# First stage of a two-layer diffusion step: small loads on ScalarE's queue, large loads reordered, first modulation and norm given priority

## The chip, the cores and the metric

The kernel runs on one core of one Trainium2 chip. The time is device microseconds of one execution; the median of several is given. The five engines of the core are named as in the profile: PE (TensorE, matmuls; its weight loads are PEld), DVE (VectorE), ACT (ScalarE), POOL (GpSimd) and SP (SyncE). SP only issues transfers. ACT, too, can issue transfers, from its own instruction stream and into a queue of its own.

## What is computed

One inference step of a hybrid network, two layers, float32, on 128 context tokens and 256 latent tokens of 1024 features (the two streams, 384 token columns together). Cut to what matters here:

```python
def trunk_layer(x, cond, lp, ctx_cache, rope_a, rope_b):
    mod = (jax.nn.silu(cond) @ lp["w_mod"] + lp["b_mod"])[:, None, :]
    sh1, sc1, g1, sh2, sc2, g2 = jnp.split(mod, MOD_CHUNKS, axis=-1)
    h = rms_norm(x, lp["norm1"]) * (1 + sc1) + sh1
    o, new_ctx = token_mixers(h, lp, ctx_cache, rope_a, rope_b)
    x = x + g1 * o
    h = rms_norm(x, lp["norm2"]) * (1 + sc2) + sh2
    x = x + g2 * conv_ffn(h, lp)
    return x, new_ctx
...
h = jnp.sin(freq[0] * (z @ w1 + b1))
h = jnp.sin(freq[1] * (h @ w2 + b2))
h = (h @ w3).reshape(L, 2, HY_ORDER, HY_CH)
```

`token_mixers` has two attentions and a long convolution (Hyena) behind one projection `w_in`. The last three lines are the head of `hyena_filters`: the filters of the long convolution depend on weights alone, not on the tokens; behind these lines they are windowed, normed and brought to the frequency domain.

## The kernel before

Tokens lie feature-major (features on the partitions, 384 token columns in the free direction). Every large product is three float32r passes (`mm3`, L267 to L269): a weight is split by ACT (L229) and DVE (L233) into a high and a low part. Weights come in blocks of 1 MB into a ring of two raw places, all of them loaded by SP.

The program is written as generators ("lines" of work), which `weave` interleaves; the order in which things are written is their priority. A scheduler then lays the instructions out on each engine by a timeline of its own, in the order of priority among what it takes to be ready. On the chip each engine runs its list strictly in order. `urgent(line, by)` gives the steps of a line the priority of instructions written `by` places earlier. A transfer takes one of eight semaphores ("lanes", DMAHW0 to 7) in turn, and before a lane is used again the issuing engine waits until its former transfer has landed. The lanes are shared by all queues.

The first stage (L1409 to L1455) makes everything that the first projection needs:

- `load_vecs` (L328): per-layer vectors, as rows, turned by PE: first freq, b1, b2 (L336, turned at L341), then b_mod, the norms, the short convolution (L333), then the FFN's convolution (L333 again, turned at L357 and L358).
- `filters(0, ...)` (L479): `t_z`, `w1`, `w2` loaded at L485 to L487; two layers of sine (`reduce_sin`, L465, seven DVE instructions and one Sin on ACT, L475); then for each of two halves of the channels and two orders `prep` (sums and differences of w3 on DVE, L236, rounding on ACT, L229), `taps` (PE L550, window on DVE L236), `sizes` (ACT L568) and `spectra` (PE L585, L593, L605). `half_inputs` (L492) loads 1.13 MB for a half (w3 four times 128 KB, the window, the bias) at L497 to L500 in rows of 1 KB; L524 loads a table of 640 KB.
- `mod_vec(0, 0)` and `mod_vec(0, 1)` (L371): shift and scale of the first norm, four blocks of 1 MB of `w_mod` each (`mod_load`, L368), multiplied at L377 with Silu of the conditions (turned at L301, Silu at L1437), then turned and biased (L236, L239).
- `load_x` (L313): PE turns the tokens (L301), DVE copies them (L318), ACT squares (L309), DVE sums.
- `norm_h` (L412): row sums (L421), reciprocal root (L403, L404), a broadcast by PE (L427), then per 128 features a product on DVE (L236), scale and shift on ACT (L435) and the split into two parts of `h` (L442, L236, or L229 and L233).

After that `hyena_in` starts the first projection (L267 to L269 with `h` and `split`), and the rest of the filters and the next modulation vectors (`mod_vec(0, 2)` first) are woven in.

## Time and profile before

| | |
|---|---|
| median of 3 runs | 1530.9 us (1530.8 to 1531.94) |
| span of the profiled execution, first to last instruction | 1528.9 us |
| median less span | 2.0 us |
| PE busy | 1484.3 us, 97% |
| DVE busy | 1014.6 us, 66% |
| ACT busy | 756.9 us, 50% |
| POOL busy | 91.1 us, 6% |
| transfers | 210 MB, mean 137 GB/s |
| mean granted clock of PE | 0.991 |

The profiled execution has no time of its own beside its span, so the 2.0 us that lie around the span are the difference to the median of the runs. Times in rows are microseconds from the span's start. A row of a timeline gives start, duration, engine, line, operation, tiles and, in brackets, the idle time before it with what the profile takes for its releaser. Busy time of PE counts pipelined matmuls, so a busy PE is not one at its peak.

### The profile page before, as it was taken

The numbers are of one execution on the slowest core, as the hardware profiler recorded it, in microseconds if no ns is written. First come the engines' busy times: TensorE is split into PE (matmuls) and PEld (weight loads), VectorE is DVE, ScalarE is ACT, GpSimd is POOL, SyncE is SP. The second block draws the span as 40 slices with busy tenths as digits, with TensorE's granted clock in tenths as the row PEclk, the third lists the DMA queues.
The fourth block names the chain that finished last, engine by engine and source line by source line (L and its number), as shares of the span: only waits on it lengthen the run. The fifth ranks groups of instructions, "written<-read, shape, count | busy, mean of one in ns | idle before, by whom it ended". The sixth has DMA issues, their size and how long they took to land.

```text
span 1528.9 us, 22323 instructions
## 1 busy us (share of the span) xinstructions
PE 1484.3 (97%) x8615; PEld 1349.2 (88%) x8615; DVE 1014.6 (66%) x1946; ACT 756.9 (50%) x1388; POOL 91.1 (6%) x120
## 2 busy tenths in 40 slices
PE   5999999999999999999999999999999999999997
PEld 2698799898779799999997988998887989999997
DVE  6868577455456796686776767874564767567674
ACT  3644365445454663453545444855454455344343
POOL 1113110000000000000000212000000000000000
PEclk9899999999999999999999999999999999999999
DMA  8634454334456533343265445242242424333531
GB/s 276 235 109 140 142 179 142 105 107 137 141 166 220 172 111 111 110 131 128 90 224 196 138 133 180 89 123 76 72 138 97 166 97 138 121 114 111 165 108 58
DMA packets 182448, 210.05 MB, mean 137 GB/s; under 512 B 25940, under 2 KB 166470, under 8 KB 182342
## 3 DMA queue, kind: packets, MB, share of 16 engines
q1 hardware_dynamic: 182342, 208.63, 42.2%
q8 instruction: 68, 1.11, 0.3%
q14 instruction: 38, 0.31, 0.1%
HBM read 206.48 MB, written 2.13 MB: 136 GB/s over the span
## 4 chain that ended last, share of the span: by engine, by line
PE 90%; DVE 3%; DMA 3%; ACT 2%; issue 1%; SPq 0%; DVEq 0%; ACTq 0%
PE banks L267 26%; PE banks L269 25%; PE banks L268 25%; PE banks L301 4%; PE banks L377 3%; PE banks L975 2%; PE banks L1003 2%; DVE s L236 1%; DMA base<-in_w_in_dram 1%; ACT s L229 1%; PE banks L605 1%; DMA s<-in_t_kdft_dram 1%; DVE split L233 1%; PE banks L550 1%; PE banks L991 0%
## 5 line engine op out<-in xcount | busy, mean ns | idle before, releaser
L229 ACT ACTIVATE split<-base 128x1024 fp32r<-128x1024 f32 (+2 forms) x272 | 280.1, 1040 | 347.6 <-PE banks L268 261.3
L233 DVE TENSOR_TENSOR split<-base,split 128x1024 fp32r<-128x1024 f32 (+2 forms) x272 | 328.5, 1214 | 168.4 <-ACT split L229 162.9
L267 PE MATMUL banks<-h,split 128*128 128x384 f32 x1280 | 435.9, 344 | 4.5 <-DVE h L442 2.5
L268 PE MATMUL banks<-h,split 128*128 128x384 f32 x1280 | 436.5, 341 | 0.6 <-DVE h L236 0.6
L269 PE MATMUL banks<-h,split 128*128 128x384 f32 x1280 | 432.6, 339 | 0.0
L267 PEld LDWEIGHTS banks<-h,split 128*128 128x128 f32 x1280 | 241.8, 189 | 20.3 <-issue 9.8
L268 PEld LDWEIGHTS banks<-h,split 128*128 128x128 f32 x1280 | 242.0, 189 | 5.6 <-issue 1.6
L269 PEld LDWEIGHTS banks<-h,split 128*128 128x128 f32 x1280 | 241.7, 189 | 2.8 <-issue 1.1
L268 PE MATMUL banks<-s,split 128*128 128x384 f32 x672 | 226.1, 337 | 0.0
L269 PE MATMUL banks<-s,split 128*128 128x384 f32 x672 | 225.0, 337 | 0.0
L267 PE MATMUL banks<-s,split 128*128 128x384 f32 x672 | 222.2, 340 | 1.0 <-ACT s L229 0.9
L229 ACT ACTIVATE s<-banks 128x384 f32<-128x384 f32 (+10 forms) x268 | 116.6, 464 | 155.0 <-PE banks L301 64.0
L239 DVE SCALAR_TENSOR_TENSOR s<-banks,base,s 128x127 f32<-128x127 f32 (+1 forms) x448 | 173.1, 410 | 10.2 <-ACT s L456 6.1
L267 PEld LDWEIGHTS banks<-s,split 128*128 128x128 f32 x672 | 125.5, 188 | 6.2 <-issue 2.3
L269 PEld LDWEIGHTS banks<-s,split 128*128 128x128 f32 x672 | 126.1, 188 | 3.3 <-DVE split L233 1.7
L229 ACT ACTIVATE s<-s 128x384 fp32r<-128x384 f32 (+4 forms) x142 | 81.9, 581 | 93.4 <-DVE s L236 47.1
L268 PEld LDWEIGHTS banks<-s,split 128*128 128x128 f32 x672 | 126.2, 188 | 0.5
L236 DVE TENSOR_TENSOR s<-banks,s 128x512 f32<-128x512 f32 (+3 forms) x132 | 81.5, 643 | 35.8 <-PE banks L269 17.3
L239 DVE SCALAR_TENSOR_TENSOR base<-banks,base 128x128 f32<-128x128 f32 (+1 forms) x128 | 46.9, 412 | 81.0 <-PE banks L269 81.0
L301 PE MATMUL banks<-base,s 128*128 128x128 f32 (+2 forms) x483 | 85.0, 276 | 5.6 <-DMA s<-in_hy_short_b_dram 4.2
L301 PEld LDWEIGHTS banks<-base,s 128*128 128x128 f32 (+2 forms) x483 | 60.1, 141 | 26.0 <-issue 9.7
L233 DVE TENSOR_TENSOR s<-s,s 128x512 fp32r<-128x512 f32 (+3 forms) x102 | 66.9, 658 | 20.8 <-ACT s L229 20.5
(151 smaller groups left out, 1741.1 us busy)
## 6 DMA issues: line engine op xcount, KB each, us to landing
base<-in_w_in_dram SPq DMA_DIRECT2D x40, 1024.0 KB
base<-in_ffn_up_dram SPq DMA_DIRECT2D x40, 1024.0 KB
base<-in_w_mod_dram SPq DMA_DIRECT2D x28, 1024.0 KB
s<-in_w_mod_dram SPq DMA_DIRECT2D x14, 1024.0 KB
base<-in_ffn_down_dram SPq DMA_DIRECT2D x16, 896.0 KB
base<-in_w_branch_dram SPq DMA_DIRECT2D x24, 512.0 KB
base<-in_w_out_dram SPq DMA_DIRECT2D x8, 1024.0 KB
base<-in_ffn_down_dram SPq DMA_DIRECT2D x8, 1024.0 KB
```

Source lines behind the costliest of these rows:

```text
L229: act.activation(out=out, in_=in_, func=AF.Copy, scale=scale)
L233: dve.tensor_tensor(out=lo, in0=src, in1=f(hi), op=ALU.subtract)
L236: dve.tensor_tensor(out=out, in0=a, in1=b, op=op)
L239: dve.scalar_tensor_tensor(out=out, in0=a, scalar=s, in1=b, op0=op0, op1=op1)
L267: pe.matmul(out, l[0], r[0], start=start, stop=False)
L268: pe.matmul(out, l[0], r[1], start=False, stop=False)
L269: pe.matmul(out, l[1], r[0], start=False, stop=stop)
L301: pe.transpose(out, in_, ident[:n, :n])
L377: pe.matmul(gv[32 * j:32 * j + 32], cT[:, 2 * k + j // 2], raw[:, j // 2, (j % 2) * 512:(j % 2) * 512 + 512], start=k == 0, stop=k == KD / ...
L550: pe.matmul(p.rearrange("p a b -> p (a b)"), hp[q].ap()[:, sl], ws.ap(), start=q == 0, stop=q == 1)
L975: pe.matmul(out, q_of(h)[:, i * 128:(i + 1) * 128], k, start=m == 0, stop=m == len(ks) - 1)
L1003: pe.matmul(po[b:b + 64], vs_of(h, n), pTs[h].ap()[:, n], start=n == 0, stop=n == 2, tile_position=(0, b))
```

## The change

It does four things, all in the first stage.

1. The small loads of the first layer (identity, `t_z`, `w1`, `w2`, the conditions and all vectors of `load_vecs(0)`) are issued by ACT instead of SP.
2. SP's large loads come in another order: the first half of the filter inputs and the table, two blocks of `w_mod`, the tokens, two blocks of `w_mod`, the second half of the filter inputs, four blocks of `w_mod`. Before, one block of `w_mod` went ahead of the filter inputs.
3. The two modulation vectors and `load_x` are written as `urgent` by 60 places.
4. The first norm is written as `urgent` by 250 places.

The diff without the comments and docstrings that it also drops:

```diff
+U_M0, U_N0 = 60, 250
...
     def load_vecs(l):
...
+        q = act if l == 0 else sp
+
         def rows(i, r0, n, src):
-            sp.dma_start(out=s[i][r0:r0 + n, :], in_=src.rearrange("(r p) -> r p", p=128))
+            q.dma_start(out=s[i][r0:r0 + n, :], in_=src.rearrange("(r p) -> r p", p=128))
 
         for r0, n, src in ((0, 2, hy_freq[l]), (2, 1, hy_b1[l:l + 1]), (3, 1, hy_b2[l:l + 1])):
-            sp.dma_start(
+            q.dma_start(
...
     def filters(l, R, spec, first=False):
...
-        sp.dma_start(out=zt.ap(p1=17), in_=t_z)
-        sp.dma_start(out=w1.ap(p1=17), in_=hy_w1[l])
-        sp.dma_start(out=w2.ap(p1=64), in_=hy_w2[l].unsqueeze(1).to_broadcast([64, 2, 64]))
+        dq = act if first else sp
+        dq.dma_start(out=zt.ap(p1=17), in_=t_z)
+        dq.dma_start(out=w1.ap(p1=17), in_=hy_w1[l])
+        dq.dma_start(out=w2.ap(p1=64), in_=hy_w2[l].unsqueeze(1).to_broadcast([64, 2, 64]))
...
-    sp.dma_start(out=ident, in_=t_ident)
+    act.dma_start(out=ident, in_=t_ident)
...
     next(vl[0])
+    cst = FA.alloc(128)
+    act.dma_start(out=cst.ap(128, p1=8), in_=c_ctx.rearrange("(k p) -> k p", p=128))
+    act.dma_start(out=cst.ap(128, p0=8, p1=16), in_=c.rearrange("o (k p) -> (o k) p", p=128))
     next(fl)
     next(fl)
-    cst = FA.alloc(128)
-    sp.dma_start(out=cst.ap(128, p1=8), in_=c_ctx.rearrange("(k p) -> k p", p=128))
-    sp.dma_start(out=cst.ap(128, p0=8, p1=16), in_=c.rearrange("o (k p) -> (o k) p", p=128))
-    ready = [mod_load(0, 0, 0, early[0])]
     next(fl)
-    next(vl[0])
-    for k in (1, 2):
-        ready.append(mod_load(0, 0, k, early[k]))
+    ready = [mod_load(0, 0, k, early[k]) for k in range(2)]
     for i, src in enumerate((x_prompt[0], x_sample[0, 0:128], x_sample[0, 128:256])):
         sp.dma_start(out=xin[i].ap(), in_=src)
+    for k in range(2, 4):
+        ready.append(mod_load(0, 0, k, early[k]))
+    next(vl[0])
     next(fl)
-    for k in range(3, KD):
-        ready.append(mod_load(0, k // 4, k % 4, early[k]))
+    for k in range(4, KD):
+        ready.append(mod_load(0, 1, k % 4, early[k]))
...
-    weave(chain(mod_vec(0, 0, ready[:4]), mod_vec(0, 1, ready[4:])), (fl, R_F0), (load_x(xin), 1.2))
+    weave(
+        urgent(chain(mod_vec(0, 0, ready[:4]), mod_vec(0, 1, ready[4:])), U_M0),
+        (fl, R_F0), (urgent(load_x(xin), U_M0), 1.2),
+    )
...
-    finish(norm_h(0, 0))
+    finish(urgent(norm_h(0, 0), U_N0))
```

What the scheduler makes of it stands below at three places. Lines of the changed kernel are some 1 to 7 higher for the same statement (L377 becomes L380, L550 becomes L554, L605 becomes L609, L267 to L269 become L268 to L270). The names are memory slabs; `split` and `h` first hold early blocks of `w_mod`. The number in brackets is a lane's.

The head of the transfer queues. SP before:

```order
L1411 DMA base_98<-in_t_ident_dram 128x128
L485 DMA s_1_109<-in_t_z_dram 17x384
L486 DMA s_1_110<-in_hy_w_dram 17x64
L487 DMA s_1_110<-in_hy_w_dram 64x2x64
L336 DMA s_1_110<-in_hy_freq_dram 2x2x64
L336 DMA s_1_110<-in_hy_b_dram 1x2x64 x2
L1423 DMA s_1_110<-in_c_ctx_dram 8x128
L1424 DMA s_1_110<-in_c_dram 8x128 [waits DMAHW0_49]
L368 DMA base_98<-in_w_mod_dram 128x2x1024 [waits DMAHW1_49]
L497 DMA s_1_146<-in_hy_w_dram 64x2x256 [waits DMAHW2_49]
```

ACT now:

```order
L490 DMA s_1_110<-in_hy_w_dram 17x64
L491 DMA s_1_110<-in_hy_w_dram 64x2x64
L339 DMA s_1_110<-in_hy_freq_dram 2x2x64 [waits DMAHW1_49]
L339 DMA s_1_110<-in_hy_b_dram 1x2x64 [waits DMAHW3_49]
L339 DMA s_1_110<-in_hy_b_dram 1x2x64 [waits DMAHW5_49]
L1425 DMA s_1_110<-in_c_ctx_dram 8x128 [waits DMAHW7_49]
...
L336 DMA s_1_110<-in_hy_short_b_dram 12x128 [waits DMAHW3_49]
L478 ACT_TABLE_LOAD
L478 ACTIVATE s_1_123<-s_1_123 64x384 [waits DVE_49]
L230 ACTIVATE s_1_142<-s_1_184 128x512 x2
L336 DMA s_1_110<-in_ffn_conv_w_dram 88x128 [waits DMAHW5_49]
...
L1441 ACT_TABLE_LOAD [waits PE_49]
```

SP now:

```order
L501 DMA s_1_145<-in_hy_w_dram 64x2x256 x2
L503 DMA s_1_145<-in_t_win_dram 128x3x256
L501 DMA s_1_145<-in_hy_w_dram 64x2x256
L501 DMA s_1_145<-in_hy_w_dram 64x2x256 [waits DMAHW0_49]
L504 DMA s_1_145<-in_hy_bias_dram 128x2x256 [waits DMAHW2_49]
L528 DMA s_1_152<-in_t_kdft_dram 128x1280 [waits DMAHW4_49]
L371 DMA base_98<-in_w_mod_dram 128x2x1024 [waits DMAHW6_49]
L371 DMA base_98<-in_w_mod_dram 128x2x1024 [waits DMAHW0_49]
L1432 DMA s_1_109<-in_x_prompt_dram 128x1024 [waits DMAHW2_49]
```

SP's first entry is now a large load, and each of the two queues reuses a lane after four loads of its own instead of eight. ACT issues fourteen small loads before its first table load and three more before its second; there was one table load at this place before.

PE from the start to the first filter taps (L550, now L554). Before:

```order
L507 MATMUL banks<-s_1_109,s_1_110 64x384
L301 MATMUL banks<-base_98,s_1_110 128x4
L301 MATMUL banks<-base_98,s_1_110 128x16
L377 MATMUL banks<-base_98 32x512 x4
L511 MATMUL banks<-s_1_121,s_1_110 128x384
L301 MATMUL banks<-base_98,s_1_110 128x112
L377 MATMUL banks<-base_98 32x512 x4
L550 MATMUL banks<-s_1_140 128x512 x8
```

Now:

```order
L511 MATMUL banks<-s_1_109,s_1_110 64x384
L302 MATMUL banks<-base_98,s_1_110 128x4
L515 MATMUL banks<-s_1_123,s_1_110 128x384
L302 MATMUL banks<-base_98,s_1_110 128x16
L302 MATMUL banks<-base_98,s_1_109 128x128
L380 MATMUL banks<-base_98 32x512 x8
L302 MATMUL banks<-base_98,s_1_109 128x128
L302 MATMUL banks<-base_98,s_1_110 128x128 x4
L554 MATMUL banks<-s_1_142 128x512 x8
```

The second sine layer (L515) no longer stands behind a block of `w_mod`; the first transposes of the tokens (L302, 128x128) now stand ahead of the taps, around the two blocks of `w_mod`.

PE at the start of the first projection. Before:

```order
L550 MATMUL banks<-s_1_140 128x512 x6
L585 MATMUL banks<-base_98,s_1_146 128x1 x6
L267 MATMUL banks<-h_418,split_417 128x384 x3
L377 MATMUL banks<-base_98 32x512 x4
L605 MATMUL banks<-s_1_121,s_1_153 128x256 x4
L268 MATMUL banks<-h_418,split_417 128x384
```

Now:

```order
L554 MATMUL banks<-s_1_142 128x512 x4
L589 MATMUL banks<-base_98,s_1_145 128x1 x6
L380 MATMUL banks<-base_98 32x512 x4
L609 MATMUL banks<-s_1_123,s_1_152 128x256 x4
L268 MATMUL banks<-h_418,split_417 128x384 x3
L269 MATMUL banks<-h_418,split_417 128x384
```

The block of `w_mod` for the third modulation vector and four spectra matmuls moved ahead of the first product with `h`. The instructions ahead of these rows are the same in kind and number as before, in another order.

## Rows read from the trace of the kernel before

**Rows 1.** Busy by stretch: us, PE, PEld, DVE, ACT, POOL, PEclk, DMA share, GB/s.

```profile
70.00:200.00 130.00, 130.00 (x748) 112.78 (x747) 85.25 (x151) 58.00 (x102) 27.80 (x34) 1.00 0.42 137
```

**Rows 2.** Busy time by stretch, from the first taps' eviction to two ends.

```profile
25.25:58.12 32.87, 29.59 (x173) 18.65 (x171) 31.37 (x62) 22.62 (x43) 6.75 (x7) 1.00 0.89 290
25.25:63.64 38.39, 34.02 (x189) 22.60 (x187) 36.89 (x72) 24.05 (x47) 9.43 (x10) 0.93 0.92 305
```

**Rows 3.** Timeline of PE.

```profile
4.48 1.51 PE L507 MATMUL banks<-s,s 17*64 17x384 f32 x2 [4.48 <-DMA s<-in_hy_w_dram]
5.92 0.66 PE L301 MATMUL banks<-base,s 4*128 4x4 f32 x2
...
18.67 0.42 PE L301 MATMUL banks<-base,s 112*128 112x112 f32 x1 [4.20 <-DMA s<-in_hy_short_b_dram]
21.39 1.93 PE L377 MATMUL banks<-base 128*32 128x512 f32 x8 [2.29 <-DMA base<-in_w_mod_dram]
23.25 2.65 PE L550 MATMUL banks<-s 128*128 128x512 f32 x8
...
63.70 1.33 PE L267 MATMUL banks<-h,split 128*128 128x384 f32 x3 [0.17 <-DVE h L442]
64.95 1.94 PE L377 MATMUL banks<-base 128*32 128x512 f32 x8
```

**Rows 4.** Timeline of SP, the transfer queue's issues.

```profile
0.73 0.40 SPq L1411 DMA_DIRECT2D base<-in_t_ident_dram  x1
1.20 0.32 SPq L485 DMA_DIRECT2D s<-in_t_z_dram  x1
1.56 0.23 SPq L486 DMA_DIRECT2D s<-in_hy_w_dram  x1
...
2.62 0.44 SPq L336 DMA_DIRECT2D s<-in_hy_freq_dram  x1
3.10 1.32 SPq L336 DMA_DIRECT2D s<-in_hy_b_dram  x2
...
5.27 0.41 SPq L368 DMA_DIRECT2D base<-in_w_mod_dram  x1
...
14.69 0.30 SPq L333 DMA_DIRECT2D s<-in_hy_short_b_dram  x1
...
58.15 0.40 SPq L368 DMA_DIRECT2D base<-in_w_mod_dram  x1
```

**Rows 5.** Busy time by stretch, for the transfers' rate.

```profile
10.00:14.00 4.00, 3.04 (x10) 0.73 (x10) 0.80 (x3) 1.15 (x2) 0.00 (x0) 1.00 1.00 243
18.00:26.00 8.00, 5.03 (x21) 2.40 (x25) 3.77 (x9) 1.04 (x2) 0.00 (x0) 1.00 1.02 403
```

**Rows 6.** Timeline of DVE, first sine layer's first and last instruction.

```profile
6.21 0.16 DVE L342 COPY base<-banks 128x4 f32<-128x4 f32 x1 [6.21 <-PE banks L301]
...
9.64 0.35 DVE L474 TENSOR_SCALAR s<-s 64x384 f32<-64x384 f32 x1
```

**Rows 7.** Timeline of ACT.

```profile
6.67 1.28 ACT L1437 ACT_TABLE_LOAD   x1 [6.67 <-PE banks L301]
7.96 0.20 ACT L1437 ACTIVATE base<-banks 128x16 f32<-128x16 f32 x1
10.03 0.52 ACT L475 ACTIVATE s<-s 64x384 f32<-64x384 f32 x1 [1.87 <-DVE s L474]
13.30 0.63 ACT L229 ACTIVATE s<-s 128x512 fp32r<-128x512 f32 x1 [2.75 <-DVE s L236]
```

**Rows 8.** Groups of DVE instructions in 25.2 to 63.4: count, busy us, mean ns, idle before.

```profile
L236 DVE TENSOR_TENSOR s<-base,banks 128x384 f32<-128x384 f32 x4 | 2.0, 540 | 0.0
L239 DVE SCALAR_TENSOR_TENSOR base<-base 128x16 f32<-128x16 f32 x1 | 1.4, 1411 | 0.0
```

**Rows 9.** Chain of waits that ended last, its piece of 8.32: start, us, what.

```profile
8.32 6.99 DMA s<-in_hy_w_dram
```

**Rows 10.** Busy time by stretch, after the fall of PE's clock.

```profile
63.70:68.82 5.12, 5.12 (x16) 2.67 (x17) 4.20 (x12) 5.12 (x12) 0.52 (x1) 0.50 0.33 101
```

## The prediction

> **What bounds the kernel now.** I read the busy time by stretch first. From 70 us on PE has no idle time, 130.00 of 130 us [rows 1], and over the whole span it is busy for 97%. What follows the first stage is bound by PE, so a microsecond won in the first stage is won at the end, if PE starts its unbroken work that much earlier with the same work left. That start is at 63.70, where the first product with `h` begins, released by DVE [rows 3].
>
> So the question is what holds DVE. From 25.25, its first eviction of a filter tap, to 63.64, the end of the first cast to `h`, DVE is busy 36.89 of 38.39 us [rows 2]: it is the bound of this stretch, with 1.50 us of idle time. Transfers, PE and ACT are mostly ahead of it. What starts the stretch is the third step: PE's taps at 23.25 stand behind a block of `w_mod` at 21.39, for which PE had waited 2.29 us [rows 3]. That block came late because SP spent its first 4.54 us on small loads, the first large one being issued at 5.27 and not at 0.73 [rows 4], and because the transfer engines were then full.
>
> **The change, part by part.** The sum goes along one path: small loads, sine layer, Silu, two blocks of `w_mod`, first DVE work, first `h`. L is the time from the issue of a small load to its first use.
>
> *Small loads on ACT.* The order shows a chain: with two queues sharing eight lanes, each small load waits for the landing of the fourth before it. No row shows two queues at once, so L is bounded: 2.16 us for the last of L336 (second half of 3.10 to 4.42, so 3.76 to 5.92), 2.92 us for L486 (1.56 to 4.48), 3.98 us for L333 behind a full queue (14.69 to 18.67) [rows 3, 4], and 6.99 us for a w3 load deep in the queue [rows 9]. I take 3.0, near 2.92, because it is the row of the same small loads with little ahead of them; in the change the large loads are in another queue. Then freq waits for the identity, 0.73 + 3.0 = 3.73, and takes 0.44; b1 waits for `t_z` until 4.20 and takes 0.66 to 4.86; b2 goes at 4.86 and can be used at 7.86 [rows 4]. PE turns it in 0.66 [rows 3], DVE's first sine layer takes 3.78 (6.21 to 9.99) [rows 6]: 12.3. Before it was 9.99, so this part loses 2.3 us. DVE's four sums of w3, now ahead of the layer, are no bound: their last load goes out when SP's first has landed, at 3.7, and is there before 7.
>
> *ACT's list.* Sin takes 0.52 and two roundings 0.63 each [rows 7]: 14.1. The fourteen loads ahead are done by then: the last waits for b_mod, which waits for b1, so 4.20 + 6.0 = 10.2, with 0.30 for itself [rows 4], and the table load of 1.28 [rows 7] ends at 11.8, under DVE's layer. The three loads behind the roundings go out at once (the latest waits for the short convolution's weights, 9.73 + 3.0 = 12.7) and take 0.9 at 0.30 each: 15.0. A second table load, which is new, brings 16.3, Silu 16.5. If the cover of the first table load goes, it costs its 1.28.
>
> *A rule weighed.* Silu started at 7.96, straight behind the table load that ended at 7.95 [rows 7]: a load costs 1.28. The Trainium skill ("ScalarE: Activation LUTs", section "What ACT_TABLE_LOAD costs") adds a drain of 1.38 us to every switch, 2.66 in all. By that the new load would cost 1.38 more and the forecast would be 1528.3; the row shows no such gap, and I go by the row.
>
> *Large loads reordered.* Two blocks of `w_mod` take 1.93 each on PE [rows 3]: 16.5 + 3.9 = 20.4. They and the tokens must be there. Ahead of and with them SP sends 1.21 MB in rows of 1 KB, at 243 GB/s 5.0 us, and 0.66 + 2.10 + 1.57 MB in longer rows, at 403 GB/s 10.7 us [rows 5]. From 0.73 and about 1.5 for the start this is 18, so PE does not wait for them; before, the second block alone came at 21.39. The rest of the first transposes lets DVE begin at about 20.8, with the copies of the tokens, against 25.25: 4.4 earlier. The second sine layer, which no longer stands behind a block on PE, is finished before that. The later blocks of `w_mod` and of `w_in` follow in the same stream some 4 us earlier and are hidden by DVE's list as before.
>
> *DVE's stretch.* The order has the same instructions ahead of the first `h` as before, and one more product with the root, 0.54 [rows 8] (and one on four columns, not costed). So 36.89 + 0.54 and the same idle 1.50 [rows 2]: 38.9, and the first `h` stands at 59.7, 3.9 earlier.
>
> *PE's start.* On PE the next block of `w_mod` and four spectra products moved ahead of the first product with `h`. They don't need `h`; the block needs its load, which SP issues when DVE has split the second raw block of `w_in`. That point was 58.12, 31.37 us of DVE work in [rows 2]; four products of 0.54 now come behind it and one of 1.41 ahead of it [rows 8], so 30.6, with 1.5 idle 52.9. From issue to use it took at most 6.80 (58.15 to 64.95) [rows 3, 4]: 59.7. A bound below is the 2.6 us that 1 MB takes at 403 GB/s [rows 5], but then PE would only be early for work ahead of `h`. So PE's unbroken work starts at 59.7, not 63.70, with the same work left: 4.0 us. Rope loads, which are unchanged, and issue time on ACT, which is idle there, I cost at nothing; the cover is ACT's idle time before its first Sin (10.03, [rows 7]).
>
> *The sum.* 1528.9 - 4.0 = 1524.9 of span, and 2.0 around it: **1526.9**, 0.26% below the median. About 0.2%, 3.1 us, is what a measurement of this kernel can tell from no change.
>
> *The ends.* With L at 2.16 the same chain starts DVE at 19.1, where the tokens' arrival nearly binds: 1525.2. With 3.98 it starts at 22.9: 1529.0. With 6.99, at 34.8: 1540.9.
>
> **The rivals.**
>
> *The chain of small loads eats most of the gain* (L about 4, 1529.0). For it: four loads in flight in place of eight, and every link counts nearly threefold (b2, then the short convolution's weights, then the FFN's three loads ahead of Silu). Against it: the loads that showed 3.98 had large ones ahead in their own queue. 22%.
>
> *The chain makes it slower.* Same place, larger price: if a small load beside a full stream takes what the w3 load took, 6.99 [rows 9], DVE starts at 34.8, 9.5 later than before, and the time is 1540.9. Between 3.98 and 6.99 each 0.1 us of L costs 0.4; the change breaks even at 4.5 and is slower by 3.1 from 5.2 on. Against it: that load had a whole block and smaller ones ahead in its queue. By the Trainium skill ("DMA: Bandwidth & Descriptors", section "Queues, rings and completion order") each transfer engine takes turns between queues packet by packet, which would keep L small; no row here shows two queues. 9%.
>
> *PE's clock.* The granted clock was 0.50, 1.2 and not 2.4 GHz, in the 5.12 us from 63.70, and PE was never idle in them [rows 10]. If this slow stretch falls ahead of PE's unbroken work or does not come, up to 2.56 us more are won: 1524.3. If it lasts as much longer, 2.56 are lost, which is about the first rival's time. PE waits for DVE ahead of its unbroken work as before, so I take the clock as it was. 12% for the gain.
>
> *The change does not do what it says.* By the order the norm's first row sums do not come ahead of filter work on PE, and the list of PE is also arranged anew far behind the first stage, where there is no idle time to win and a stall of a microsecond or two can be met: about 1528.5 to 1530. 7%.
>
> **How the numbers follow.** The forecast with L between about 2.5 and 3.6 has 50%. Faster by over 0.2%: most of the forecast (0.44), the clock's gain (0.12) and a little of the rest, 0.58. Within 0.2%: the first rival, the last and the upper end of the forecast, 0.33. Slower: 0.09. The range goes from 1522.6, the short L with the clock's gain, to 1532.0, where L is 4.7; beyond lies most of the second rival.
>
> **What would show it.** Right: the first large load is issued below 1 us; DVE copies tokens from about 21; Silu at 16 to 17; the first product with `h` within 60 to 63 and PE unbroken from about 60; the difference at 70 us is the difference at the end. Wrong: small loads on ACT with more than 4 us from issue to use, Silu behind 19, PE waiting for the block of `w_mod` with `h` ready, or new idle time of PE behind 70.

## The result and the profile after

The change is **slower**: 1545.65 us, median of 4 runs (1542.18 to 1547.32), against 1531.1 us before (4 runs on the same chip), a ratio of 1.0088 [1.0074, 1.0102], so 14.5 us. The forecast was 1526.9 us, its range ended at 1532.0. The profiled execution took 1546.93 us, its span is 1545.1 us, 16.2 more than before.

**The first stage after.** ACT's queue (ACTq rows are the issues of loads, ACT rows its instructions; start, duration, idle time before):

```profile
3.87 0.25 ACTq L339 DMA_DIRECT2D s<-in_hy_freq_dram  x1
5.14 1.33 ACTq L339 DMA_DIRECT2D s<-in_hy_b_dram  x2
8.27 0.28 ACTq L1426 DMA_DIRECT2D s<-in_c_dram  x1
8.59 0.86 ACTq L336 DMA_DIRECT2D s<-in_b_mod_dram  x1
9.49 1.65 ACTq L336 DMA_DIRECT2D s<-in_norm_dram  x2
14.84 0.30 ACTq L336 DMA_DIRECT2D s<-in_hy_short_w_dram  x1
15.37 0.30 ACTq L336 DMA_DIRECT2D s<-in_hy_short_b_dram  x1
15.71 1.28 ACT L478 ACT_TABLE_LOAD   x1 [15.71 <-DMA s<-in_norm_dram]
17.00 0.52 ACT L478 ACTIVATE s<-s 64x384 f32<-64x384 f32 x1
20.33 1.28 ACT L1441 ACT_TABLE_LOAD   x1 [1.77 <-DMA s<-in_hy_short_w_dram]
21.62 0.20 ACT L1441 ACTIVATE base<-banks 128x16 f32<-128x16 f32 x1
```

The short convolution's weights take the lane that c had taken, so their issue at 14.84 says when c landed: 6.57 us after 8.27. Behind them stands Sin, whose input DVE had finished at 12.97 (its last row starts at 12.62 and takes 0.35). Sin comes at 17.00, Silu at 21.62; before it was 10.03 and 7.96 [rows 7]. PE in the same stage, and where the first products with `h` begin:

```profile
8.91 0.24 PE L302 MATMUL banks<-base,s 4*128 4x4 f32 x1 [1.39 <-DMA s<-in_hy_b_dram]
17.58 1.64 PE L515 MATMUL banks<-s,s 64*128 64x384 f32 x2 [8.43 <-ACT s L478]
21.88 3.64 PE L380 MATMUL banks<-base 128*32 128x512 f32 x16 [2.04 <-ACT base L1441]
26.43 2.76 PE L554 MATMUL banks<-s 128*128 128x512 f32 x8
...
66.27 1.93 PE L380 MATMUL banks<-base 128*32 128x512 f32 x8 [0.23 <-DMA base<-in_w_mod_dram]
68.13 3.78 PE L609 MATMUL banks<-s,s 128*128 128x256 f32 x8
71.35 1.30 PE L268 MATMUL banks<-h,split 128*128 128x384 f32 x3
```

The taps come at 26.43 in place of 23.25, and PE's unbroken work at 66.27 in place of 63.70 [rows 3]: 2.6 later, where 4.0 earlier was forecast. The stretches of [rows 1, 2] in the trace after:

```profile
26.60:67.20 40.60, 36.54 (x198) 24.30 (x197) 34.97 (x74) 26.15 (x51) 10.47 (x10) 0.89 0.77 257
70.00:200.00 130.00, 129.83 (x713) 109.81 (x712) 83.97 (x152) 57.87 (x103) 28.89 (x32) 0.99 0.40 129
```

DVE is busy 34.97 of the 40.60 us from its first copy into the first cast to `h` (66.90 to 67.42), and no longer without gaps. From 70 to 200 us PE is busy nearly all the time, as before. So most of the loss comes behind the first stage. Over all that follows 70 us, before and after:

```profile
70.00:1528.90 1458.90, 1434.21 (x8378) 1319.44 (x8376) 962.16 (x1839) 722.21 (x1320) 80.33 (x100) 0.99 0.41 131
70.00:1545.10 1475.10, 1447.35 (x8387) 1325.70 (x8385) 962.81 (x1844) 726.15 (x1325) 87.47 (x100) 0.99 0.41 130
```

PE is idle for 24.7 us there before and for 27.8 after. So 3.1 us are new waiting, and the rest is PE's work, which takes longer. Two things are seen in it.

**Blocks in pieces.** A modulation block is four matmuls of 32 columns of the array (two rows each, L377 before, L380 after). In the trace after, one block of the first layer stands like this among other products (PE, start and duration):

```profile
190.62 1.04 PE L380 MATMUL banks<-base 128*32 128x512 f32 x2
191.59 0.39 PE L269 MATMUL banks<-s,s 128*128 128x256 f32 x1
...
192.03 1.04 PE L380 MATMUL banks<-base 128*32 128x512 f32 x2
...
195.32 1.04 PE L380 MATMUL banks<-base 128*32 128x512 f32 x2
...
197.44 1.04 PE L380 MATMUL banks<-base 128*32 128x512 f32 x2
```

Each piece holds PE for 0.97 us until the next product starts (190.62 to 191.59). A whole block of the same weights, from the run joined_change below:

```profile
188.46 1.07 PE L381 MATMUL banks<-base 128*32 128x512 f32 x8
189.46 0.38 PE L268 MATMUL banks<-s,s 128*128 128x256 f32 x1
```

Four matmuls one behind the other hold PE for 1.00. So each piece beyond the first costs nearly a block. In the scheduler's order of before 9 of the 48 blocks are cut in two (57 pieces), in that of the change 61 pieces stand. The groups of PE by line from 70 to 330 us, before and after (busy us, mean ns of one row):

```profile
L377 PE MATMUL banks<-base 128*32 128x512 f32 x88 | 13.8, 605 | 0.0
```

```profile
L380 PE MATMUL banks<-base 128*32 128x512 f32 x88 | 17.9, 605 | 0.0
```

The same 88 rows of the same length, less overlapped: 4.1 us more. Over the whole span (these lines alone: us, busy time of PE and PEld, then clock, DMA share, GB/s), before and after, it is 5.0 more:

```profile
0.00:1528.90 1528.90, 60.42 (x384) 10.20 (x384) 0.99 0.43 137
0.00:1545.10 1545.10, 65.39 (x384) 10.85 (x384) 0.99 0.43 136
```

The Trainium skill ("TensorEngine Tiling (Array Packing)", section "Tiling Modes") says that tiles run in parallel and that a change of tiling mode drains the engine. The rows agree with the first: four tiles together take 1.00, one by itself 0.97. No row here sets a drain apart.

**The clock.** The granted clock was 0.50 in seven stretches, before in four. After the same gap of PE, in the middle of the first layer, before and after (windows: busy us of PE, PEld, DVE, ACT, POOL, then clock, DMA share, GB/s):

```profile
350.00:362.00 12.00, 9.86 (x64) 9.13 (x63) 6.87 (x13) 6.24 (x11) 0.00 (x0) 1.00 0.40 125
```

```profile
359.00:371.00 12.00, 9.86 (x52) 8.68 (x51) 6.08 (x12) 6.12 (x10) 0.00 (x0) 0.86 0.38 115
```

PE is as busy in both, with the same wait of 2.14 us for ACT ahead of the products at 352.90 and 361.73; the clock fell to 1.2 GHz for a while in the second alone. Over the span the mean granted clock was 0.9918 (mean of 96 runs of before, taken beside the experiments) and 0.9882 after (4 runs). The share by which it is below 1, times the span, is what the lower clock can cost at most, and is called the clock cost below: 12.6 us before, 18.1 after. The mean times are 1531.6 and 1545.2, so at least 8 of the 13.6 us between them are left to other causes.

### The profile page after: what moved, and what is told of

Same layout as the page of the kernel before. It is cut to its first block, busy times and chain, and to the rows that moved or that the text cites. A ratio compares the mean times of both kernels' runs of the same rounds, so it can differ in the third digit from the quotient of the medians.

```text
span 1545.1 us, 22309 instructions
## 1 busy us (share of the span) xinstructions
PE 1495.4 (97%) x8615; PEld 1354.6 (88%) x8615; DVE 1010.9 (65%) x1946; ACT 760.5 (49%) x1389; POOL 98.7 (6%) x120
## 4 chain that ended last, share of the span: by engine, by line
PE 91%; DMA 3%; DVE 2%; ACT 2%; issue 1%; SPq 0%; POOL 0%; DVEq 0%; ACTq 0%; POOLq 0%
PE banks L268 26%; PE banks L270 25%; PE banks L269 25%; PE banks L302 4%; PE banks L380 4%; PE banks L979 2%; PE banks L1007 2%; DMA base<-in_w_mod_dram 1%; PE banks L609 1%; ACT s L230 1%; DMA s<-in_t_kdft_dram 1%; DVE split L234 1%; PE banks L554 1%; PE banks L995 0%; DMA s<-in_c_dram 0%
## 5 line engine op out<-in xcount | busy, mean ns | idle before, releaser
L268 PE MATMUL banks<-h,split 128*128 128x384 f32 x1280 | 434.5, 343 | 4.5 <-DVE h L445 2.3
L269 PE MATMUL banks<-h,split 128*128 128x384 f32 x1280 | 436.5, 341 | 0.0
L270 PE MATMUL banks<-h,split 128*128 128x384 f32 x1280 | 433.2, 339 | 0.7 <-DVE split L234 0.7
L268 PEld LDWEIGHTS banks<-h,split 128*128 128x128 f32 x1280 | 242.5, 190 | 19.9 <-issue 8.8
L269 PEld LDWEIGHTS banks<-h,split 128*128 128x128 f32 x1280 | 241.9, 189 | 4.7 <-issue 1.1
L270 PEld LDWEIGHTS banks<-h,split 128*128 128x128 f32 x1280 | 241.8, 189 | 4.1 <-issue 1.3
L269 PE MATMUL banks<-s,split 128*128 128x384 f32 x672 | 226.5, 338 | 0.0
L270 PE MATMUL banks<-s,split 128*128 128x384 f32 x672 | 225.4, 338 | 0.0
L268 PE MATMUL banks<-s,split 128*128 128x384 f32 x672 | 222.2, 340 | 1.0 <-ACT s L230 0.9
L240 DVE SCALAR_TENSOR_TENSOR s<-banks,base,s 128x127 f32<-128x127 f32 (+1 forms) x448 | 172.4, 411 | 15.5 <-ACT s L459 11.7
L268 PEld LDWEIGHTS banks<-s,split 128*128 128x128 f32 x672 | 125.4, 188 | 6.5 <-issue 2.3
L270 PEld LDWEIGHTS banks<-s,split 128*128 128x128 f32 x672 | 126.2, 188 | 3.3 <-DVE split L234 1.7
L269 PEld LDWEIGHTS banks<-s,split 128*128 128x128 f32 x672 | 126.3, 188 | 0.4
L302 PE MATMUL banks<-base,s 128*128 128x128 f32 (+2 forms) x483 | 84.9, 278 | 4.0 <-DMA s<-in_hy_b_dram 1.4
L302 PEld LDWEIGHTS banks<-base,s 128*128 128x128 f32 (+2 forms) x483 | 60.0, 141 | 27.5 <-issue 12.4
L459 ACT ACTIVATE s<-banks,base 128x384 f32<-128x384 f32 x112 | 73.4, 656 | 17.7 <-PE banks L270 17.7
```

Source lines behind the costliest of these rows:

```text
L240: dve.scalar_tensor_tensor(out=out, in0=a, scalar=s, in1=b, op0=op0, op1=op1)
L268: pe.matmul(out, l[0], r[0], start=start, stop=False)
L269: pe.matmul(out, l[0], r[1], start=False, stop=False)
L270: pe.matmul(out, l[1], r[0], start=False, stop=stop)
L302: pe.transpose(out, in_, ident[:n, :n])
L459: act.activation(out=dst, in_=src, func=AF.Identity, scale=vec(l, w1), bias=vec(l, bias))
```

## The experiments

Times are medians; each run has its own runs of before beside it (1531.1 to 1532.0). "Joined" kernels have whole blocks (below). "Pieces" counts the unbroken parts of the 48 blocks in the scheduler's order.

| kernel | us | ratio to before | pieces | mean clock cost |
|---|---|---|---|---|
| change | 1545.65 | 1.0088 [1.0074, 1.0102] | 61 | 18.1 |
| change_no_urgency | 1543.54 | 1.0081 [1.0065, 1.0097] | 61 | 17.9 |
| urgency_only | 1538.31 | 1.0045 [1.0032, 1.0057] | 61 | 12.3 |
| start_06_later | 1538.71 | 1.0050 [1.0036, 1.0064] | 61 | 14.5 |
| start_34_later | 1535.30 | 1.0027 [1.0016, 1.0039] | 57 | 13.6 |
| late_start | 1531.64 | 1.0004 [0.9995, 1.0013] | 57 | 14.1 |
| joined_before | 1527.07 | 0.9970 [0.9958, 0.9981] | 48 | 12.6 |
| joined_urgency | 1527.95 | 0.9978 [0.9969, 0.9986] | 48 | 13.9 |
| joined_change | 1529.42 | 0.9993 [0.9983, 1.0004] | 48 | 16.6 |
| joined_loads_on_SP | 1532.79 | 1.0010 [1.0001, 1.0020] | 48 | 15.6 |
| joined_ACT_only | 1532.02 | 1.0002 [0.9991, 1.0013] | 48 | 16.1 |
| joined_rows_on_POOL | 1527.27 | 0.9971 [0.9959, 0.9983] | 48 | 16.3 |
| joined_loads_on_POOL | 1543.91 | 1.0086 [1.0072, 1.0100] | 48 | 20.8 |
| joined_c_first | 1548.62 | 1.0115 [1.0101, 1.0129] | 48 | 25.1 |
| joined_rows_behind | 1536.64 | 1.0030 [1.0018, 1.0042] | 48 | 21.3 |
| joined_rows_apart | 1525.21 | 0.9968 [0.9954, 0.9983] | 48 | 13.9 |
| joined_rows_apart_old | 1529.89 | 0.9983 [0.9972, 0.9993] | 48 | 12.8 |

### What cut blocks cost

**Whole blocks.** The edit, in before and in the change alike:

```diff
             for j in range(4):
-                pe.matmul(
+                with tc.high_priority(offset=100000 if j else 0), tc.issue_after(mm.ins) if j else ExitStack():
+                    mm = pe.matmul(
```

The second to fourth matmul of a block go straight behind the first; nothing else of the program is touched. (The scheduler draws the first stage of the change anew even so: the taps come at 24.1 in place of 26.43, PE's unbroken work at 66.73 in place of 66.27.)

> The kernel before, with the four column-packed matmuls of each modulation block issued one behind the other, so that no other matmul stands between them. Theory (pieces): in the trace of before and of the change a block takes 1.00 us as one piece, and each piece takes 0.98 when other matmuls stand between. The order of before cuts 9 of its 48 blocks in two (57 pieces), so 9 x 0.98 = 8.8 us go: 1522.3, within 1.5. Rival (pieces cost nothing at the end, since other work fills the gaps or the clock sets the time): 1531.1 within 1.

> The change with the same edit. Its order has 61 pieces of 48 blocks. Theory (three terms: pieces about 4 us more than before, a later first h 2.7 us, half-clock stretches that fall at other places for the rest, about 8): 13 x 0.98 = 12.7 go, 1532.9 within 2; against the joined version of before 2.7 from the first stage stay and up to 8 from the clock. Rival (all of the 14.5 us comes from the first stage and from what it shifts, the pieces are without weight): 1545.6 within 2.

Measured: 4.4 us faster than its runs of before, and, for the change, 16.2 less than the change itself (1545.65 to 1529.42). In the change the theory is right in sign, and 3.5 us more came back than it said, which is outside its 2. In before half as much came back as expected. There the blocks hold PE for 51.69 us in place of 60.42, as the theory has it, but PE waits more: behind 70 us it is idle for 27.9 in place of 24.7. A part of that shows around 838 us, in the second layer's first projection. PE in the joined version of before:

```profile
838.85 0.30 PE L301 MATMUL banks<-base,s 128*128 128x128 f32 x1 [0.85 <-DVE s L239]
...
840.53 0.69 PE L269 MATMUL banks<-h,split 128*128 128x384 f32 x1 [0.96 <-DVE split L233]
```

In before the like of the second product stands at 844.48, and PE had no idle time from 834 to 846. With whole blocks the change costs 2.4 us against before, not 14.5: **12 of the 14.5 us hang on the cut blocks**, in part through what they shift.

**The urgency by itself, and the change without it.** The first adds `urgent` of the diff to before, with its loads untouched; the second sets `U_M0, U_N0 = -1, -1` in the change.

> The kernel before with nothing of the change but the urgency (60 and 250); all loads as before. In its order the first stage is that of before up to the first products with h, and nothing differs ahead of them; behind them the blocks are cut as in the change, 61 pieces of 48 blocks in place of 57. Theory (pieces and clock, whatever brings another order behind the first stage): 4 x 0.98 = 3.9 slower than before, and up to 4 more where half-clock stretches follow: 1534 to 1539, with no difference at 70 us. Rival (the loss is made by the loads in the first stage and only carried along): 1531.4 within 1.

> The change with its urgency taken out (both offsets -1), not joined. In the order the lists of PE and DVE differ from those of the change in a few rows near the first norm, those of SP, ACT and POOL in none, and the blocks are cut into the same 61 pieces. Theory (the moved loads already make the planner draw that order, and the urgency adds nothing to it): the same as the change, 1545.6 within 2. Rival (the two parts add up, 7 us of the loss belong to the urgency): 1538.6 within 2.

Measured: 1538.31, 7.0 us slower with loads that have not changed and PE's unbroken work from 64.23, only 0.5 later than in before. The clock has no part in it (its cost is that of before, 12.3). The group of L377 from 70 to 330 us is busy 18.0 us, as in the change:

```profile
L377 PE MATMUL banks<-base 128*32 128x512 f32 x88 | 18.0, 605 | 0.0
```

Without urgency the change takes 1543.54, 2.1 less than with it, within the spread of the runs of either (1542.9 to 1546.9, 1542.2 to 1547.3). The two parts don't add up: either of them makes the scheduler draw an order with 61 pieces, and one of them is enough. With the same 61 pieces the moved loads cost some 5 us more than the urgency, and their clock cost is 5.6 higher (17.9 and 12.3).

**Urgency with whole blocks.** Both edits together.

> The joined version of before with the urgency (60 and 250) added; loads as before. The urgency alone cost 7 us with the first stage unchanged. Theory (it is the cut blocks that cost, not the other order as such): with whole blocks nothing of it is left, the same as the joined version of before, 1527.1 within 1.5. Rival (the other order costs by itself, by stalls of PE): 1530 or more.

Measured: 1527.95, within 0.9 of the joined version of before. The theory holds: another order costs next to nothing here, cut blocks do.

**Only a later start.** All loads in the order of before, the first behind one or eleven memsets of its destination on POOL:

```diff
+    for _ in range(1):
+        pool.memset(ident, 0.0)
...
-    sp.dma_start(out=ident, in_=t_ident)
+    hold = tc.issue_after(sp.dma_start(out=ident, in_=t_ident).ins)
```

(`hold` spans the program, so that no load of SP's overtakes this one.)

> The kernel before with nothing but its start put off: SP's first load, the identity, waits for one memset of it on POOL, and all later loads stay behind it, in the order of before. SP starts at about 1.4 in place of 0.73. The planner, which reckons with that, arranges the list of PE anew behind the first stage: 61 pieces in place of 57. Theory (any shift of the first stage lets the planner draw another order, and the order of before is one with few cut blocks): 0.7 for the shift and 4 to 7 for the pieces as with the urgency alone: 1536 to 1539. Rival (the order has no weight): 1532.1 within 0.8.

> The same edit with eleven memsets, SP starts at about 4.1 in place of 0.73. Here the planner draws the very order of before, 57 pieces. Theory (a late start is carried to the end as it is when the order stays): 1531.4 + 3.4 = 1534.8 within 1.2, less than the 0.7 us shift with the other order. Rival (half-clock stretches come after other gaps when everything is later): more than 1.7 us beside that, to either side, with stretches after gaps that had none in before.

Measured: with PE's first product 0.6 us later (5.05, in before 4.48) the time is 7.3 us longer, with 3.4 later it is 3.9. Of the 7.3, 2.1 stand already at the start of PE's unbroken work (65.78 and 63.70). In the second the list is that of before. I wrote the order out for one to twelve and for fourteen memsets: 61 pieces nine times, 62 once, 57 three times (ten to twelve memsets). So the order of before is a fortunate draw, and a shift of the reckoned times by one memset is enough to make the scheduler draw again.

In the profiled execution of the second, the product behind the gap shown above starts 3.5 us later than in before (356.38 and 352.90), but its like in the second layer only 1.0 later (1097.45 and 1096.43): a half-clock stretch that before had between them did not come. Windows of before and of this kernel, 10 us each:

```profile
823.00:833.00 10.00, 7.15 (x30) 5.65 (x27) 8.90 (x19) 8.77 (x20) 0.00 (x0) 0.68 0.73 245
```

```profile
826.00:836.00 10.00, 6.75 (x46) 3.96 (x38) 8.90 (x19) 8.85 (x20) 0.00 (x0) 1.00 0.71 243
```

With the same order and a start 3.4 us later, PE was idle a little longer in this window (3.25 us for 2.85), and no fall followed. The rival, too, is right in part: the length of the waits alone does not settle whether the clock falls after them. What else does is not shown.

**A first try at the shift** put the memsets elsewhere.

> The kernel before, its whole work about 1.7 us later and in the same order: seven memsets on POOL ahead of the identity's load, which SP's queue then waits for. Theory (whether a gap on PE brings a half-clock stretch depends on when it comes, so a shift alone changes their sum): the time moves by the shift plus or minus 1 to 4 us, and the stretches behind 70 us come after other gaps or in another number than in before (826.6 to 833.4 and 1239.6 to 1243.0). Rival (the stretches belong to the gaps themselves, and a shift changes nothing): 1531.4 + 1.7 = 1533.1 within 0.6, with the same stretches.

It missed: the scheduler put the identity's memset ahead of the others, the work moved by 0.3 to 0.4 us only, and the half-clock stretches with it. It tells nothing of a shift of 1.7.

### What the first stage costs

All of these have whole blocks.

**Loads or order alone.** The joined change with its small loads back on SP (`act` and `q` back to `sp`), and the joined version of before with its small loads on ACT.

> The joined change with its small loads back on SP's queue: the new order of the large loads and the urgency stay. Theory (the small loads on ACT are what delays the first stage, by a chain over shared lanes): SP has issued the small loads by 5.3, the sine layers are done by about 15, two modulation blocks are on PE by about 16.5, DVE begins its evictions at 17 to 20 and not at 25.3 or 26.6, first h at 57 to 60, PE unbroken 4 to 6 us earlier than in before: 1516 to 1519. Rival (the order of the large loads is what delays it, tokens and w_mod stand behind w3 and the DFT table): first h at 66 or later and a time as the joined change.

> The joined version of before with nothing but its small loads put on ACT's queue; the order of the large loads and of the norm as before. Theory (chain over shared lanes): the last small load that the first sine layer needs lands near 9 and c near 15, Silu near 21 as in the change, DVE's evictions from 26 to 28, first h at 66 to 68: 2 to 5 us slower than the joined version of before, 1524 to 1527. Rival (the order of the large loads is at fault): Silu before 12 and no slower than the joined version of before, 1522.

Measured: both slower than the joined change by their medians (3.4 and 2.6 us; their intervals still overlap with its own), and my theory falls for the first: its first products with `h` come at 73.5. SP there (queue SPq), and PE:

```profile
16.88 0.33 SPq L336 DMA_DIRECT2D s<-in_b_mod_dram  x1
19.43 2.84 SPq L336 DMA_DIRECT2D s<-in_norm_dram  x2
...
25.82 3.11 SPq L501 DMA_DIRECT2D s<-in_hy_w_dram  x2
...
34.15 0.98 SPq L371 DMA_DIRECT2D split<-in_w_mod_dram  x2
```

```profile
42.96 1.07 PE L381 MATMUL banks<-split,base 128*32 128x512 f32 x8 [3.08 <-DMA split<-in_w_mod_dram]
```

The row loads stand behind tokens and four blocks of `w_mod`; each waits for a lane that a large load holds, and with it all of SP's stream. The blocks of `w_mod` at 34.15 are waited for. The rival named the order of the large loads: it is that order with small loads in the same lanes. The small loads alone on ACT were 4.9 slower than the joined version of before, at the upper end of what was expected (Silu at 18.9, first products at 72.3).

**Lanes of their own.** Small loads on POOL's queue. It has eight lanes of its own; those named at the start are shared by SP and ACT alone. All of them went there (in the joined change), or only the eight row loads (in the joined version of before).

> The joined change with its small loads on POOL's queue, where they have eight lanes of their own and SP keeps its eight. Theory (the two queues' shared lanes are what delays the first stage of the change): the first eight small loads go without a wait, c lands by about 9, SP's stream is not held up by small loads, DVE begins its copies of the tokens at 15 to 22, first h at 58 to 63 in place of 66.9 and PE unbroken 4 to 8 us earlier than in the joined change: 1522 to 1526. Rival (the new order of the large loads is itself the delay, as in the joined change with the loads on SP): first h at 65 or later, 1529 or more.

> The joined version of before, with only the eight loads of row vectors (b_mod, norms, short convolution, FFN convolution) put on POOL's queue; the order of the large loads and the head of PE's list as before. In before five of them stand on SP from 10.84 to 14.99, each waiting for a lane, ahead of the second block of w_mod at 15.32. Theory (they hold up SP's stream): that block is issued at 10.3 to 11, PE no longer waits 2.29 us for it ahead of the taps, DVE's evictions start at 22 to 23.5 and not at 25.25, first h at 60 to 62: 1.5 to 3.5 faster than the joined version of before, 1523.5 to 1525.5. Rival (the transfer engines are full anyway, so an earlier issue lands no earlier): 1527 within 1.

Measured: 1543.91 and 1527.27. Neither theory is settled by the first, for the scheduler moved the second sine layer on PE behind four blocks and most of the tokens, and its taps come at 37.45:

```profile
19.80 0.45 PE L302 MATMUL banks<-base,s 128*128 128x128 f32 x1 [8.56 <-DMA s<-in_x_prompt_dram]
...
30.97 0.91 PE L515 MATMUL banks<-s,s 64*128 64x384 f32 x2
...
37.45 3.78 PE L554 MATMUL banks<-s 128*128 128x512 f32 x8 [4.45 <-ACT s L230]
```

It shows one thing: the prompt's tokens, issued at 6.17 with no small load in its lanes, were there at 19.80 only. The second is clearer. SP, then PE:

```profile
10.96 0.37 SPq L368 DMA_DIRECT2D base<-in_w_mod_dram  x1
```

```profile
20.06 1.94 PE L378 MATMUL banks<-base 128*32 128x512 f32 x8 [5.09 <-DMA base<-in_w_mod_dram]
```

The second block of `w_mod` was issued 4.4 us earlier than in before (15.32) and used 1.3 earlier (21.39 [rows 3]). The first product with `h` started at 62.82, 0.9 earlier than in before, and the time at the end is that of the joined version of before. The rival holds for the loads: the transfer engines are full, and an earlier issue mostly waits longer. That an earlier start is worth nothing does not follow: ahead of 70 us PE was idle 1.2 us less than in the joined version of before (18.9 and 20.2), and the clock cost was 3.7 higher.

**c first.** Its two loads at the head of ACT's queue.

> The joined change with the two loads of c at the head of ACT's queue, ahead of the identity. In the change c is issued at 8.27, lands at about 14.8 and holds Silu until 21.6. Theory (that one late load is what makes the first stage late): c lands by 4, Silu by 8, the first two blocks of w_mod are on PE at 13 to 17 in place of 21.9, first h at 60 to 64 in place of about 66, 2 to 5 us faster than the joined change: 1524.5 to 1527.5. Rival (the transfer engines are full, and tokens, w3 and w_mod land no earlier): first h at 65 or later, 1528 or more.

Measured: 1548.62, far slower. The theory is wrong; the rival's numbers hold, but not its reason. ACT:

```profile
1.36 0.29 ACTq L1417 DMA_DIRECT2D s<-in_c_dram  x1
...
14.67 0.30 ACTq L336 DMA_DIRECT2D s<-in_hy_short_w_dram  x1
...
16.22 1.28 ACT L1441 ACT_TABLE_LOAD   x1 [16.22 <-DMA s<-in_norm_dram]
17.51 0.20 ACT L1441 ACTIVATE base<-banks 128x16 f32<-128x16 f32 x1
```

PE had turned c by 4.62, yet Silu came at 17.51: what holds it is **not c but ACT's own list**, on which fourteen loads stand ahead of it, each waiting for a lane. (Sin was put behind it and came at 27.01, and so the taps at 40.3.)

**Row loads out of ACT's way.** Behind Silu (under `tc.issue_after(silu.ins)`), or on POOL's queue, the latter with both orders of the large loads:

```diff
-            q.dma_start(out=s[i][r0:r0 + n, :], ...
+            (pool if l == 0 else sp).dma_start(out=s[i][r0:r0 + n, :], ...
```

> The joined change with b_mod, the norms and the short convolution's weights loaded on ACT behind Silu in place of ahead of Sin. Theory (a, ACT's list): Sin no longer waits from 12.97 to 15.7 or 17.0 for the loads ahead of it, nor Silu to 19.5; but the three FFN loads still stand ahead. Sin at 13 to 15, Silu at 16 to 18, first taps at 20 to 23 in place of 24.1, first h at 62 to 66 in place of 67.3: 1525 to 1528. Theory (b, transfers are full): first h at 66.5 or later and 1529.4 within 1.5.

> The joined change with all eight row loads on POOL's queue and lanes, so that ACT carries only the nine small loads that the first stage needs at once, and Sin and Silu have no wait for a lane ahead of them. Theory (a): Sin at 13 to 14, Silu at 15 to 16.5, first taps at 19 to 21.5 in place of 24.1, first h at 61.5 to 64.5 in place of 67.3: 1523.5 to 1527. Theory (b): first h at 66 or later, 1528 or more.

> The same (nine small loads on ACT, eight on POOL) with the order of the large loads of before and no urgency. Theory (the new order of the large loads brings w3 and the DFT table earlier than the first block of w_mod and is worth 1 to 2 us): first h 1 to 2 us later than in joined_rows_apart, 1525 to 1528. Rival (what is loaded first is all the same since all has to land before the norm): the same as joined_rows_apart within 1.

Measured: 1536.64, **1525.21** and 1529.89. Behind Silu the loads hold up the next instruction, the second Sin; ACT there:

```profile
15.92 0.20 ACT L1440 ACTIVATE base<-banks 128x16 f32<-128x16 f32 x1
21.36 0.33 ACTq L336 DMA_DIRECT2D s<-in_b_mod_dram  x1
24.21 4.67 ACTq L336 DMA_DIRECT2D s<-in_norm_dram  x2
...
31.70 0.52 ACT L478 ACTIVATE s<-s 128x384 f32<-128x384 f32 x1 [15.58 <-DMA s<-in_norm_dram]
```

DVE had finished that Sin's input at 19.99, so 11.7 of the 15.58 us are idle time of an engine that had work: what (a) says of ACT's list is shown, though in the other direction. Off ACT altogether, the time is 4.2 less than the joined change. It is the fastest of all, ahead of the joined version of before by 1.9, which their intervals don't separate. But not by the steps I gave: Silu was 17.57 and the taps still 24.0 (c, issued at 9.11, was used at 14.21), the first cast of `h` 56.7, since here the scheduler put the norm ahead of filter work, and the first products with `h` 67.1 against 71.8. With the old order of the large loads (and no urgency) the median was 4.7 higher, more than the 1 to 2 expected, but the intervals overlap. Its first product with `h` came 1.5 earlier (65.62), not later; its first sine layer began on PE at 10.06 in place of 6.08, and PE was idle 25.8 us ahead of 70 in place of 22.3. What the order of the large loads is worth by itself is not shown.

## Why the prediction was wrong

1. **What bounds the kernel**: right in the main, but read too far. [rows 1] ends at 200 us. Behind 70 PE was idle for 24.7 us in before, and for 27.8 after. New idle time there was one of the signs of being wrong, and it came, as did c's 6.57 us and Silu behind 19.
2. **Small loads, the chain to b2**: right. b2 could be used at 8.91, forecast 7.86; the sine layer was done at 12.97, forecast 12.3. L was 3.1 there (its issue, half of 5.14 to 6.47, to 8.91).
3. **ACT's list: this step failed first.** "The fourteen loads ahead are done by then" took L = 3.0 for every link. From c on it was 6.57, for by then SP's large loads filled the transfer engines (7.23 of the 7.52 MB moved in the first 25 us were SP's). The last of the fourteen went at 15.37, not 10.2; Sin waited 4.0 us with its input ready (12.97 to 17.00), 1.28 of them for the table load, whose cover was gone, and Silu came 5.1 late (21.62 for 16.5). The second rival had the price, 6.99 from [rows 9], and the place, but as a price of all links; the trace had some 3 for the first links and 6.6 from c on. The rule that I set against it, that each transfer engine takes turns between queues (the Trainium skill, "DMA: Bandwidth & Descriptors", section "Queues, rings and completion order"), would keep L small; c's 6.57 beside a full queue does not bear that out.
4. **Large loads**: "PE does not wait for them" held because Silu came so late. But their transfers were held to be free of the small ones, and they share lanes: SP had four at a time, and its stream ended no earlier than before (the seventh and eighth block of `w_mod` issued at 31.16, before at 30.04).
5. **DVE's stretch**: it began at 26.60, not 20.8, with 34.97 us of work for 37.4 forecast, but with 5.6 us of gaps in place of 1.5. With (3), PE's unbroken work began at 66.27, 6.6 later than forecast, as soon as its block of `w_mod` was there (issued at 60.98, forecast 52.9). Behind that start the half-clock stretch of [rows 10], which began at 58.6 in both, reached to 72.3 in place of 68.8; that costs up to 1.7 more.
6. **"With the same work left"**: this step failed by most. I read from [rows 1] that a microsecond at 64 us is one at the end, and read the order near the three places of the sum only. The last rival did name a list arranged anew behind the first stage, at 7% and with "a stall of a microsecond or two". New waits came, 3.1 us behind 70, but more of the loss is work that overlaps less, 5.0 us over the whole span, and that was no term of the sum or of a rival. With whole blocks all but 2.4 of the 14.5 us are gone. The pieces could be counted in the order, and their price stands in the trace of before, which has cut blocks too.
7. **The clock** was taken "as it was". Its cost rose from 12.6 to 18.1 us. Of this 5.5, 4.0 stay with whole blocks (12.6 and 16.6), so most of it does not come from the cuts. Between the two joined kernels the mean times differ by 3.4 (1530.5 and 1527.1), which the clock could cost alone. But PE's unbroken work starts 2.8 later there, too (66.73 and 63.95), and ahead of 70 us PE is idle for 22.4 us in place of 20.2. How much of the 3.4 is the clock and how much the first stage stays open.

The sum as measured, in the two profiled executions, whose spans are 16.2 us apart: 2.0 of new idle time of PE ahead of 70 us and 3.1 behind it, 5.0 for the cut blocks, and 6.1 of other work of PE that took longer. For the last the clock gives at most 6.3 (0.009 of 1528.9 before, 0.013 of 1545.1 after). The first stage, 4.0 earlier by the forecast, came 2.6 later. What stays open: why the clock falls after one gap and not after its like, and how much of the new waiting the cuts bring; only whole blocks as such were tried.

## What to carry to other kernels

Where a scheduler draws each engine's list from reckoned times, an edit at the start redraws all of it: compare the whole order, and look for places where neighbours matter, such as packed matmuls; pin those together before judging any edit. Loads issued by an engine that also computes belong behind nothing that waits: its list is in order, and a small load's wait for a lane becomes the wait of the next instruction. Before moving a load forward, see whether the transfer engines have room; if they are full, it mostly waits longer (here it was issued 4.4 us earlier and used 1.3 earlier).

## What was not expected of the hardware

- A column-packed matmul that stands alone holds PE for 0.97 us, four of them together for 1.00.
- With the transfer engines full, a load issued 4.4 us earlier was used only 1.3 us earlier, and 4 KB (c) took 6.57 us beside them, with as little ahead in its own queue as b2 had, which took 3.1.
- The same gap of PE, with the same 2.14 us wait, was followed by the lower clock in one kernel and not in another, and in one case a fall was gone in the same order started 3.4 us later, though the waits ahead of it were no shorter.
